# Setting up a pair of heads' operands behind the newest exponential, with the doubled copies on GpSimd

## The chip, the cores and the metric

The kernel runs on one core of one Trainium2 chip. The metric is the device time of one execution in microseconds (us). The profiler's names for the engines are used throughout: PE is TensorE (matmuls and transposes), PEld its weight loads, ACT is ScalarE, DVE is VectorE, POOL is GpSimd, and SP is SyncE, which only issues DMAs. Each engine works through its own instructions in order. POOL also issues the DMAs of its own queue, among them all gathers from the paged cache.

## The reference

One step of a decoder layer is computed for two groups that share weights: a prompt of 1024 tokens, and eight samples of one token each, which attend to 8192 cached tokens. The parts that matter here are the prompt's:

```python
q, k, v, logf, u, z = mixer_inputs(rmsnorm(xp, g_mix[l]), w_in[l], b_f[l], g_sgu_v[l])
xp = xp + merge_heads(fox_prompt(q, k, v, logf), sgu_prompt(u, z, w_s[l], b_s[l]),
                      g_att_out[l], g_sgu_out[l], w_o[l])
...
    s = jnp.einsum('bqhd,bkhd->bhqk', q, k).astype(jnp.float32) * (ATT_HEAD_DIM ** -0.5)
    s = s + (cq.astype(jnp.float32).transpose(0, 2, 1)[:, :, :, None]
             - ck.astype(jnp.float32).transpose(0, 2, 1)[:, :, None, :])
    s = jnp.where(kpos[None, :] <= qpos[:, None], s, -jnp.inf)
    p = jax.nn.softmax(s, axis=-1).astype(v.dtype)
```

There are eight heads of width 64, each with a cumulated forget gate `c` that enters the scores as a difference. Beside the attention stands a gating unit, `u * (W z + b)`, whose output is normalised by the mean of its squares. After both come an output projection, a cross-attention into 256 memory tokens, and a gated MLP.

## The kernel before, in words

The prompt is worked in stages: the input projection (`p1`), attention for the first 512 query rows (`attention(0)`), attention for the second 512 (`attention(1)`), and then, for each half, output projection, cross-attention and MLP. Beside attention of the first half, a filler generator computes the memory's keys and values (`pmem`) and the gating unit (`gating(0)`). `gating(1)` runs beside the first half's cross-attention. The decode of the samples is a background generator: a loop at the end of `build` advances it by one step whenever the main generator's yields have added up to a pace, which is 20 in the first half's attention. A step is, among other things, a gather of keys (L1354), their multiplication with the query and a sum (DVE, L1360 and L1364), and a gather of values (L1413) with matmuls (L1419).

The program's text order is not the engines' order. The framework simulates the program and orders every engine's instructions by when they become ready in that simulation, the earlier in the text first. `tc.issue_after(x)` forbids one thing: the instructions of its block may not stand ahead of `x` on `x`'s engine. `newest(e)` gives the newest instruction traced on an engine, and `behind(e)` is `issue_after` with the newest instruction of engine `e` at the main program's last yield.

Attention works on pairs of heads (`hp`, four per half), each in two blocks (`blk`) of 256 query rows, with four score tiles per block (two heads `j`, two row tiles `ii`). A score tile is a full-precision product made of two matmuls over split operands (L759, L761), plus a mask (L763). Its maximum is taken by DVE (L765, or L768 where the tile fills two PSUM banks), and the exponential with its row sum by ACT (L766, L769). The probabilities are transposed by PE (L787) and copied out of PSUM by ACT or DVE (L792, L794), and multiplied with the values (L803); the result is turned back (L823, L825). The program keeps two score tiles ahead of their transposition.

The operands of a pair come from `setup`, a generator with one yield. Its first part transposes the queries (L701) into a PSUM tile. For each head it copies the high part out twice by ACT (L707 into `qq[0:64, 0]`, L708 into `qq[0:64, 1]`), fetches the gate's rows by POOL's DMAs (L709, L721), and lets DVE subtract the high part from the PSUM tile to get the low part (L724). Its second part does the same with the keys: transposes (L729), a copy by ACT (L733), a second copy into the other 64 partitions, by ACT in the first half of the sequence (L737) and by POOL in the second (L735), and DVE's subtraction (L740). In the first half, POOL then stores both key parts to DRAM (`ks_d`, L743 and L744), from which the second half reads them. In the main loop, `setup` of the next pair starts after the last score tile of block 0 and ends one score tile later.

The first pair of each half has no pair before it. For the first half, `early` in the input projection runs the load and the whole setup; for the second half, `late` does so when pair 3 (`at`) of the first half begins. In the second half, `late` issues the loads for the following stage.

The gating unit takes the sum of squares of each of its four row tiles by ACT (`ssq_into`, L228, called once `u` has been formed), and normalises with it.

Of the kernel before, what the change touches and what calls it, by code (L numbers as in the profile page):

```python
# [7 lines left out]
F32 = mybir.dt.float32  # L8
# [3 lines left out]
AF = mybir.ActivationFunctionType  # L12
# [6 lines left out]
P = 128  # L19
# [59 lines left out]
def build(nc, tc, ctx, a, phases=None):  # L79
# [145 lines left out]
    def ssq_into(dst, src):  # L225
        n = src.shape[-1]
        j = tpool.tile([P, 1024], BF16, tag="junk", bufs=1, name=nm("junk"))[: src.shape[0], :n]
        nc.scalar.activation(j, src, AF.Square, accum_out=dst)  # L228
# [354 lines left out]
    def gating(hf):  # L583
# [6 lines left out]
        for pr_ in range(2):  # L590
# [32 lines left out]
                    )  # L623
                yield 1
            for i in range(2):
                ssq_into(ssu[:, pr_ * 2 + i : pr_ * 2 + i + 1], u[:, i, :])
            us_.append(u)
        r = rstd_of(ssu, AW, 4, "r4")
        yield 1
# [51 lines left out]
    def attention(hf, late=None, at=3):  # L681
# [14 lines left out]
            return qn, kn, vn  # L696

        def setup(hp, qn, kn, vn):
            tr = (MS, BB, BA)[SB]()
            for i in range(4):  # L700
                nc.tensor.transpose(tr[:, i * P : (i + 1) * P], qn[:, i, :], ident)  # L701
            qab, ka, kb = [], [], []
            for j in range(2):
                h = hp * 2 + j
                rows = slice(64 * j, 64 * j + 64)
                qq = U([P, 2, 512], F32R)
                nc.scalar.activation(qq[0:64, 0, :], tr[rows, :], AF.Copy)  # L707
                nc.scalar.activation(qq[0:64, 1, :], tr[rows, :], AF.Copy)  # L708
                nc.gpsimd.dma_start(qq[64:68, 1, :], cq_d[h, :, hf * 512 : (hf + 1) * 512])  # L709
                qab.append(qq)  # L710
                if hf == 0:
# [10 lines left out]
            for j, qq in enumerate(qab):  # L722
                rows = slice(64 * j, 64 * j + 64)
                nc.vector.tensor_tensor(qq[64:128, 0, :], tr[rows, :], qq[0:64, 0, :].bitcast(F32), op=ALU.subtract)  # L724
            for kh in (hf,):
                yield
                tr = (MS, BB, BA)[SB]()
                for i in range(4):
                    nc.tensor.transpose(tr[:, i * P : (i + 1) * P], kn[:, i, :], ident)  # L729
                s = slice(kh * 512, kh * 512 + 512)  # L730
                for j in range(2):
                    rows = slice(64 * j, 64 * j + 64)
                    nc.scalar.activation(ka[j][0:64, s], tr[rows, :], AF.Copy)  # L733
                    if KP & 1 << hf:
                        nc.gpsimd.tensor_copy(ka[j][64:128, s], ka[j][0:64, s].bitcast(F32))  # L735
                    else:
                        nc.scalar.activation(ka[j][64:128, s], tr[rows, :], AF.Copy)  # L737
                for j in range(2):
                    rows = slice(64 * j, 64 * j + 64)
                    nc.vector.tensor_tensor(kb[j][0:64, s], tr[rows, :], ka[j][0:64, s].bitcast(F32), op=ALU.subtract)  # L740
            if hf == 0:
                for j in range(2):
                    nc.gpsimd.dma_start(ks_d[hp * 2 + j, :, 0, :], ka[j][0:64, :].bitcast(F32))  # L743
# [3 lines left out]
        def scores(qkv, ls, blk, j, ii):  # L747
# [16 lines left out]
            if nch == 1:  # L764
                nc.vector.tensor_reduce(mx, s, axis=AX.X, op=ALU.max, negate=True)  # L765
                nc.scalar.activation(p_[:, :e], s, AF.Exp, bias=mx, accum_out=ls[:, ii, j : j + 1])  # L766
            else:
                nc.vector.tensor_reduce(mx, both, axis=AX.XY, op=ALU.max, negate=True)  # L768
                nc.scalar.activation(  # L769
                    p_[:, :e].rearrange("p (c n) -> p c n", c=2), both, AF.Exp, bias=mx, accum_out=ls[:, ii, j : j + 1]  # L770
                )
            return p_

        turns = [0.0, 0]
# [61 lines left out]
                queue.pop(0)()  # L836

        got = []
        for _ in setup(0, *load(0)):
            pass  # L840
        nxt = None
        yield 2
        for hp in range(4):
            for _ in nxt or ():
                pass
            qkv, nxt = got.pop(), None
            if hp == at and late:
                late()
            for blk in range(2):
                ls = sm([P, 2, 2], "ls", 3)  # L850
                pt = []
                nkt = hf * 4 + blk * 2 + 2
# [430 lines left out]
    def final(hf, xt, sq):  # L1283
# [7 lines left out]
                nc.sync.dma_start(a["o_y"][rows, c], xt[i][:, c])  # L1291
        yield 1

    last = {}
    bgs, acc, phase = [], [0.0], ["p1", None]

# [660 lines left out]
```

## Time and profile before

| | us |
|---|---|
| median of 3 runs | 1864.72 (1860.55 to 1866.24) |
| the profiled execution's own time | 1858.95 |
| its span, first to last instruction | 1857.2 |
| PE busy | 1779.9 |
| DVE busy | 1390.5 |
| ACT busy | 749.2 |
| POOL busy | 488.5 |
| attention, both halves | 265 to 512 |
| PE busy in attention | 211.92 of 247.00 |

A row of the profile names the source line, the engine, the operation, and the output and input tiles. In the view of waits, "A <- B" says that A's engine stood idle until B ended, with the total, the number of times and the longest. In the timeline each row has the start, the duration and, in brackets, the idle time before it and who ended it. In the view by windows each engine's busy time in a stretch is given with its number of instructions, then the clock that PE was granted as a share of full speed, and the DMA engines' share.

### The profile page before, as it was taken

The numbers are of one execution on the slowest core, as the hardware profiler recorded it, in microseconds if no ns is written. First come the engines' busy times: TensorE is split into PE (matmuls) and PEld (weight loads), VectorE is DVE, ScalarE is ACT, GpSimd is POOL, SyncE is SP. The second block draws the span as 40 slices with busy tenths as digits, with TensorE's granted clock in tenths as the row PEclk, the third lists the DMA queues.
The fourth block names the chain that finished last, engine by engine and source line by source line (L and its number), as shares of the span: only waits on it lengthen the run. The fifth ranks groups of instructions, "written<-read, shape, count | busy, mean of one in ns | idle before, by whom it ended". The sixth has DMA issues, their size and how long they took to land.

```text
span 1857.2 us, 24238 instructions
## 1 busy us (share of the span) xinstructions
PE 1779.9 (96%) x9239; PEld 1290.3 (69%) x9239; DVE 1390.5 (75%) x1666; ACT 749.2 (40%) x1365; POOL 488.5 (26%) x437
## 2 busy tenths in 40 slices
PE   8999998878998999999999999999999999999998
PEld 5887666556676757777777777766576668767765
DVE  4788567876688787989989899898975549754344
ACT  6332355565633535332324234235353334232232
POOL 1243342242122222224332232233322111111110
PEclk9999999999999999999999999999999999999999
DMA  8877889684596976768768789988879588577971
GB/s 318 291 268 262 311 302 346 230 255 150 187 400 228 349 258 262 278 249 326 293 246 339 269 312 363 360 308 338 332 275 348 198 298 266 199 270 265 342 277 60
DMA packets 157012, 521.27 MB, mean 281 GB/s; under 512 B 20808, under 2 KB 40520, under 8 KB 124128
## 3 DMA queue, kind: packets, MB, share of 16 engines
q0 software_dynamic: 57168, 341.14, 49.0%
q1 hardware_dynamic: 92816, 165.99, 25.6%
q10 hardware_dynamic: 6912, 12.59, 1.8%
q8 instruction: 73, 1.20, 0.3%
q14 instruction: 43, 0.35, 0.1%
HBM read 495.73 MB, written 23.93 MB: 280 GB/s over the span
## 4 chain that ended last, share of the span: by engine, by line
PE 67%; DVE 10%; issue 9%; DMA 9%; ACT 4%; POOL 2%; SPq 0%; POOLq 0%; DVEq 0%; ACTq 0%
PE ba L270 9%; PE ba L271 9%; PE ba L272 9%; PE dv L1419 5%; PE bb L271 5%; PE bb L270 4%; PE bb L272 4%; DMA kv<-cache_v,kidx 2%; DVE kv L1360 2%; DMA kv<-cache_k,kidx 2%; DVE s L1364 2%; PE ba L1008 1%; DVE wl L234 1%; PE ba L1010 1%; PE ba L1009 1%
## 5 line engine op out<-in xcount | busy, mean ns | idle before, releaser
L233 ACT ACTIVATE wh<-wr 128x1024 fp32r<-128x1024 f32 (+2 forms) x220 | 229.0, 1044 | 493.1 <-PE ba L271 159.3
L234 DVE TENSOR_TENSOR wl<-wr,wh 128x1024 fp32r<-128x1024 f32 (+2 forms) x220 | 262.2, 1200 | 142.2 <-PE ba L272 54.5
L1354 POOL DMA_INDIRECT kv<-cache_k,kidx x128 | 185.3, 1448 | 611.5 <-DVE s L1364 376.6
L1360 DVE TENSOR_TENSOR kv<-kv,d 128x1024 f32<-128x1024 f32 (+1 forms) x185 | 295.6, 1628 | 42.6 <-DMA kv<-cache_k,kidx 42.5
L1364 DVE TENSOR_REDUCE s<-kv 128x16 f32<-128x1024 f32 (+1 forms) x185 | 295.9, 1619 | 0.1
L1413 POOL DMA_INDIRECT kv<-cache_v,kidx x128 | 171.3, 1338 | 294.4 <-PE dv L1419 191.9
L271 PE MATMUL ba<-u,wh 128*128 128x512 f32 (+1 forms) x560 | 220.6, 394 | 2.3 <-DVE u L237 2.1
L270 PE MATMUL ba<-u,wh 128*128 128x512 f32 (+1 forms) x560 | 219.8, 394 | 1.3 <-ACT u L236 1.1
L272 PE MATMUL ba<-u,wl 128*128 128x512 f32 (+1 forms) x560 | 219.7, 393 | 0.0
L270 PE MATMUL ba<-wh,u 128*128 128x512 f32 (+1 forms) x495 | 185.6, 378 | 1.4 <-DVE u L740 1.0
L271 PE MATMUL ba<-wl,u 128*128 128x512 f32 (+1 forms) x495 | 186.3, 377 | 0.0
L272 PE MATMUL ba<-wh,u 128*128 128x512 f32 (+1 forms) x495 | 184.2, 376 | 0.0
L1419 PE MATMUL dv<-kv,s 128*32 128x512 f32 x1024 | 130.5, 618 | 7.0 <-DMA kv<-cache_v,kidx 6.8
L270 PEld LDWEIGHTS ba<-u,wh 128*128 128x128 f32 x560 | 106.0, 190 | 33.8 <-issue 9.3
L271 PEld LDWEIGHTS ba<-u,wh 128*128 128x128 f32 x560 | 106.4, 190 | 33.1 <-issue 7.1
L272 PEld LDWEIGHTS ba<-u,wl 128*128 128x128 f32 x560 | 106.3, 190 | 32.5 <-issue 10.1
L271 PE MATMUL bb<-u,wh 128*128 128x512 f32 (+1 forms) x304 | 118.2, 389 | 1.7 <-DVE u L237 1.7
L270 PE MATMUL bb<-u,wh 128*128 128x512 f32 (+1 forms) x304 | 118.0, 389 | 0.5 <-ACT u L236 0.5
L272 PE MATMUL bb<-u,wl 128*128 128x512 f32 (+1 forms) x304 | 116.8, 384 | 0.0
L270 PEld LDWEIGHTS ba<-wh,u 128*128 128x128 f32 x495 | 92.9, 188 | 26.5 <-issue 5.9
L271 PEld LDWEIGHTS ba<-wl,u 128*128 128x128 f32 x495 | 93.1, 188 | 22.2 <-issue 5.9
L272 PEld LDWEIGHTS ba<-wh,u 128*128 128x128 f32 x495 | 93.1, 188 | 19.9 <-issue 3.1
(437 smaller groups left out, 3197.5 us busy)
## 6 DMA issues: line engine op xcount, KB each, us to landing
wr<-w_up SPq DMA_DIRECT2D x88, 512.0 KB
kv<-w_up POOLq DMA_DIRECT2D x22, 1024.0 KB, 7.0
wr<-w_down SPq DMA_DIRECT2D x40, 512.0 KB
kv<-w_down POOLq DMA_DIRECT2D x11, 1024.0 KB, 8.0
wr<-w_in SPq DMA_DIRECT2D x16, 512.0 KB
wr<-w_o SPq DMA_DIRECT2D x16, 512.0 KB
wr<-w_cq SPq DMA_DIRECT2D x16, 512.0 KB
wr<-w_co SPq DMA_DIRECT2D x16, 512.0 KB
```

What stands on the lines that cost most here:

```text
L233: nc.scalar.activation(h, src, AF.Copy)
L234: nc.vector.tensor_tensor(l, src, h.bitcast(F32), op=ALU.subtract)
L270: mmul(out, sh, mh, start=(i == 0), stop=False)
L271: mmul(out, sh, ml, start=False, stop=False)
L272: mmul(out, sl, mh, start=False, stop=(i == n - 1))
L1008: mmul(pss[i], mh[k][:, tb], wh, start=(k == korder[0]), stop=False)
L1009: mmul(pss[i], mh[k][:, tb], wl, start=False, stop=False)
L1354: nc.gpsimd.indirect_dma_start(kv, None, a["cache_k"], off(kidx[:, b, ch : ch + 1]))
L1360: nc.vector.tensor_tensor(kvv[:, i : i + m, :], kvv[:, i : i + m, :], qb.unsqueeze(1).broadcast_to((P, m, 512)), op=ALU.mult)
L1364: nc.vector.tensor_reduce(s[:, ch * 4 + i : ch * 4 + i + m, :].rearrange("p k h -> p (k h)"), kvv[:, i : i + m, :].rearrange("p k (h d) -> ...
L1413: nc.gpsimd.indirect_dma_start(kv, None, a["cache_v"], off(kidx[:, b, ch : ch + 1]))
L1419: mmul(dv[32 * j : 32 * j + 32, :], s[:, ch * 4 : ch * 4 + 4, :].rearrange("p k h -> p (k h)"), kvv[:, j, :], start=(ch == 1), stop=(ch == ...
```

## The change

`lastexp` is a list that holds the newest exponential's instruction; `scores` refreshes it. The diff does these things:

- The transposes of `setup` stand behind the newest PE instruction of the main program's last yield.
- ACT's copies in `setup` (L707, L733) stand behind the newest exponential, if there is one.
- The second query copy (L708) and the first half's second key copy (L737) are made by POOL, from the first copy in SBUF instead of from PSUM. The second half's key copy was made so before.
- The squares of the gating unit stand behind the newest exponential, if there is one.
- The first pair's setup yields 2 between its query part and its key part. `early` therefore runs only the query part within the input projection, and the key part comes at the start of attention. `late` is called in both blocks of pair 3 of the first half, so that the second half's first setup has its query part in block 0 and its key part in block 1.

```diff
             for i in range(2):
-                ssq_into(ssu[:, pr_ * 2 + i : pr_ * 2 + i + 1], u[:, i, :])
+                with tc.issue_after(lastexp[0]) if lastexp else nullcontext():
+                    ssq_into(ssu[:, pr_ * 2 + i : pr_ * 2 + i + 1], u[:, i, :])
...
         def setup(hp, qn, kn, vn):
-            tr = (MS, BB, BA)[SB]()
-            for i in range(4):
-                nc.tensor.transpose(tr[:, i * P : (i + 1) * P], qn[:, i, :], ident)
+            calm = lambda: tc.issue_after(lastexp[0]) if lastexp else nullcontext()
+            with behind(ENG.PE):
+                tr = (MS, BB, BA)[SB]()
+                for i in range(4):
+                    nc.tensor.transpose(tr[:, i * P : (i + 1) * P], qn[:, i, :], ident)
             qab, ka, kb = [], [], []
             for j in range(2):
                 h = hp * 2 + j
                 rows = slice(64 * j, 64 * j + 64)
                 qq = U([P, 2, 512], F32R)
-                nc.scalar.activation(qq[0:64, 0, :], tr[rows, :], AF.Copy)
-                nc.scalar.activation(qq[0:64, 1, :], tr[rows, :], AF.Copy)
+                with calm():
+                    nc.scalar.activation(qq[0:64, 0, :], tr[rows, :], AF.Copy)
+                nc.gpsimd.tensor_copy(qq[0:64, 1, :], qq[0:64, 0, :].bitcast(F32))
                 nc.gpsimd.dma_start(qq[64:68, 1, :], cq_d[h, :, hf * 512 : (hf + 1) * 512])
...
-            for kh in (hf,):
-                yield
+            yield
+            with behind(ENG.PE):
                 tr = (MS, BB, BA)[SB]()
                 for i in range(4):
                     nc.tensor.transpose(tr[:, i * P : (i + 1) * P], kn[:, i, :], ident)
-                s = slice(kh * 512, kh * 512 + 512)
-                for j in range(2):
-                    rows = slice(64 * j, 64 * j + 64)
+            s = slice(hf * 512, hf * 512 + 512)
+            for j in range(2):
+                rows = slice(64 * j, 64 * j + 64)
+                with calm():
                     nc.scalar.activation(ka[j][0:64, s], tr[rows, :], AF.Copy)
-                    if KP & 1 << hf:
-                        nc.gpsimd.tensor_copy(ka[j][64:128, s], ka[j][0:64, s].bitcast(F32))
-                    else:
-                        nc.scalar.activation(ka[j][64:128, s], tr[rows, :], AF.Copy)
-                for j in range(2):
-                    rows = slice(64 * j, 64 * j + 64)
-                    nc.vector.tensor_tensor(kb[j][0:64, s], tr[rows, :], ka[j][0:64, s].bitcast(F32), op=ALU.subtract)
+                nc.gpsimd.tensor_copy(ka[j][64:128, s], ka[j][0:64, s].bitcast(F32))
+            for j in range(2):
+                rows = slice(64 * j, 64 * j + 64)
+                nc.vector.tensor_tensor(kb[j][0:64, s], tr[rows, :], ka[j][0:64, s].bitcast(F32), op=ALU.subtract)
...
+            lastexp[:] = [newest(ENG.Activation)]
             return p_
...
         got = []
-        for _ in setup(0, *load(0)):
+        first = setup(0, *load(0))
+        next(first)
+        yield 2
+        for _ in first:
             pass
         nxt = None
         yield 2
...
             qkv, nxt = got.pop(), None
-            if hp == at and late:
-                late()
             for blk in range(2):
+                if hp == at and late and (blk == 0 or hf == 0):
+                    late()
                 ls = sm([P, 2, 2], "ls", 3)
...
+    lastexp = []
     last = {}
```

## The prediction

> **What bounds the kernel now.** I read the page's engine table first, then the busy time by windows, then TensorE's waits in the one stage that the change touches, then the timeline at each of those waits.
>
> ```profile
> span 1857.2 us, 24238 instructions
> PE 1779.9 (96%) x9239; PEld 1290.3 (69%) x9239; DVE 1390.5 (75%) x1666; ACT 749.2 (40%) x1365; POOL 488.5 (26%) x437
> ```
>
> TensorE (PE) is busy for 96% of the span. Without removing matmuls there are about 77 us of idle time to win, and whatever the clock loses. The view by windows, first for attention as a whole (both halves, 265 to 512 us), then for its worst stretch, where one half passes into the other:
>
> ```profile
> core 0: us, PE busy (x) PEld busy (x) DVE busy (x) ACT busy (x) POOL busy (x), PEclk, DMA share, GB/s
> 265.00:512.00 247.00, 211.92 (x1317) 148.45 (x1316) 179.58 (x267) 148.22 (x328) 68.46 (x80) 0.94 0.71 244
> 365.00:396.00 31.00, 24.01 (x131) 14.29 (x133) 21.32 (x41) 19.16 (x54) 10.38 (x14) 0.83 0.71 224
> ```
>
> In attention PE idles 247.0 - 211.9 = 35.1 us, nearly half of all its idle time, and a granted clock of 0.94 costs up to 0.06 x 247 = 14.8 us more (0.17 x 31 = 5.3 us of it in the worst stretch). GpSimd (POOL) works only 68.5 of those 247 us. Whom PE waits for, in the view of waits of this window (total, times, longest):
>
> ```profile
> PE bb L787 <- ACT t L766: 8.3, 6, 2.7
> PE ba L759 <- ACT wr L769: 5.9, 4, 2.6
> PE ms L803 <- ACT t L794: 5.4, 4, 2.1
> ...
> PE bb L803 <- ACT u L794: 2.2, 3, 1.1
> ```
>
> These are 21.8 of the 35.1 us. Each names ScalarE (ACT): an exponential (L766, L769) or the copy of turned probabilities (L794) that came late. ACT works in order, so the question is what stood ahead of it.
>
> **The change part by part.** *Work taken from ACT.* The doubled query copy L708 goes to POOL for all pairs, the doubled key copy L737 for the first half (the second half has it on POOL already, L735). The groups by line, for 225 to 515 us, and the POOL copy's row:
>
> ```profile
> L708 ACT ACTIVATE u<-ba 64x512 fp32r<-64x512 f32 x16 | 9.3, 583 | 0.0
> ...
> L737 ACT ACTIVATE u<-ba 64x512 fp32r<-64x512 f32 x8 | 4.7, 592 | 0.2
> ```
>
> ```profile
> L735 POOL CAST u<-u x8: 603/607/2821, 379.6 to 471.6; 64x512 fp32r<-64x512 f32 x8
> ```
>
> So ACT loses 9.3 + 4.7 = 14.0 us and POOL gains 24 x 0.607 = 14.6 us. Since only two ACT copies then read the transposed PSUM tile before VectorE's (DVE's) subtraction, that tile comes free about 2 x 0.583 = 1.2 us earlier too. What this is worth is read at the waits. The clearest is the start of the second half, where six setup copies stand ahead of an exponential:
>
> ```profile
> 377.86 0.59 ACT L707 ACTIVATE u<-ba 64x512 fp32r<-64x512 f32 x1 [2.40 <-PE ba L701]
> ...
> 380.42 0.59 ACT L733 ACTIVATE u<-ba 64x512 fp32r<-64x512 f32 x1
> 381.03 0.37 ACT L766 ACTIVATE t<-ba,mx 128x128 f32<-128x128 f32 x1
> ```
>
> ```profile
> 378.55 0.79 DVE L765 TENSOR_REDUCE mx<-ba 128x1 f32<-128x128 f32 x2 [0.73 <-PE ba L763]
> ```
>
> ```profile
> 381.55 0.48 PE L787 MATMUL bb<-cp,t 128*128 128x128 f32 x1 [2.67 <-ACT t L766]
> ...
> 384.53 0.78 PE L759 MATMUL ba<-u,u 128*128 128x512 f32 x1
> ```
>
> The maxima of the first of the two scores were there at about 378.55 + 0.79/2 = 378.9, the exponential began at 381.03: 2.1 us late, of PE's 2.67. Here all the edits act together: two of the copies go to POOL, the others queue behind the newest exponential, and the key part of this setup moves to the next block. The other waits of this kind, PE's rows:
>
> ```profile
> 303.82 0.47 PE L270 MATMUL ba<-wh,u 128*128 128x512 f32 x1 [0.95 <-DVE u L740]
> 331.87 0.55 PE L787 MATMUL bb<-cp,t 128*128 128x128 f32 x3 [0.58 <-ACT t L766]
> 361.91 0.44 PE L787 MATMUL bb<-cp,t 128*128 128x128 f32 x2 [1.24 <-ACT t L766]
> 406.98 1.30 PE L803 MATMUL bb<-u,u 128*64 128x256 f32 x10 [1.08 <-ACT u L794]
> 437.55 1.95 PE L803 MATMUL ms<-u,u 128*64 128x256 f32 x16 [1.86 <-ACT t L794]
> 467.08 1.73 PE L803 MATMUL bb<-u,u 128*64 128x256 f32 x13 [0.89 <-ACT u L794]
> ```
>
> and an example of what stands ahead, at 437:
>
> ```profile
> 435.63 0.59 ACT L707 ACTIVATE u<-ba 64x512 fp32r<-64x512 f32 x1
> 436.13 0.58 ACT L708 ACTIVATE u<-ba 64x512 fp32r<-64x512 f32 x1
> 436.74 0.60 ACT L794 ACTIVATE u<-bb 128x512 f32<-128x512 f32 x1
> ```
>
> Each such setup puts two L708 of 0.58, together 1.17 us, ahead of the late copy, so I credit the smaller of the wait and 1.17: 0.95 + 0.58 + 1.17 + 1.08 + 1.17 + 0.89 = 5.8. With the 2.1 above, **7.9 us of waits** go. What is late next is DVE's maximum, for which the exponentials of the second half already wait:
>
> ```profile
> ACT wr L769 <- DVE mx L768: 17.0, 17, 1.9
> ```
>
> so I credit no more than the copies' own time.
>
> *The gating unit's squares* (L228, four in each half) only move behind the newest exponential. Their chain ends in a store that is read much later; the 1.24 us above already holds what their move can give: nothing extra.
>
> *The clock.* Behind the 2.67 us gap the 512-column score took 0.78 us; one at full clock took 0.47:
>
> ```profile
> 362.54 0.47 PE L759 MATMUL ba<-u,u 128*128 128x512 f32 x1
> ```
>
> If the gap goes, I take half of the worst stretch's 5.3 us back: **2.6 us**. Bounds: 0 (other gaps keep the clock down), and 14.8 for all of attention.
>
> The Trainium skill ("TensorE: Matmul & The Clock Gate", "What's actually happening") says that the clock halves after an idle window of some 3.4 us. By that rule a gap of 2.67 us would cost no clock and its removal would give none back: the sum would be 2.6 us smaller. The trace disagrees here, by its clock of 0.83 behind that gap, unless several short gaps add up.
>
> *The POOL copies as a new wait.* The query copy is now ACT, then POOL, then the scores' second matmul. Its slack, from the last L708 of a setup to the first score of the next pair:
>
> ```profile
> 330.26 0.59 ACT L708 ACTIVATE u<-ba 64x512 fp32r<-64x512 f32 x1
> ```
>
> ```profile
> 340.42 0.31 PE L759 MATMUL ba<-u,u 128*128 128x128 f32 x1
> ```
>
> 9.6 us: a copy of 0.6 us, even two, hides. But POOL also issues the cache gathers in order, and a gather holds the queue until its buffer is free:
>
> ```profile
> 458.06 0.98 POOL L1413 DMA_INDIRECT kv<-cache_v,kidx  x1 [15.40 <-DVE s L1364]
> ```
>
> A copy queued behind that one would be 15.4 - 9.6 = 5.8 us late. The other way round, a gather, or the constants' DMAs (L709, L721) behind a copy that waits for ACT, can slip; POOL's 178 idle us cover that. Copies also stretch:
>
> ```profile
> 412.75 2.82 POOL L735 CAST u<-u 64x512 fp32r<-64x512 f32 x1
> ```
>
> ```profile
> 412.75 2.34 DVE L1360 TENSOR_TENSOR kv<-kv,d 128x1024 f32<-128x1024 f32 x2
> ```
>
> One of eight did, beside the decode's multiply: 24/8 x 2.2 = 6.6 us of POOL, again under its idle time. The Trainium skill ("GPSIMD Engine Reference", "Key points") states this contention for DVE instructions with two SBUF inputs; the trace agrees, with 2.82 against 0.61 us. Between 0 and 5.8 us I take **1 us**, nearest to the eight L735 of which none was held by a gather.
>
> *The first setup's key part* moves from the projection's tail to the start of attention, with its four stores to ks_d on POOL and behind PE's newest matmul. Rows of the same operations:
>
> ```profile
> 377.66 0.60 PE L729 MATMUL ba<-cp,t 128*128 128x128 f32 x4
> ```
>
> ```profile
> L740 DVE TENSOR_TENSOR u<-ba,u 64x512 fp32r<-64x512 f32 x14 | 9.6, 685 | 6.7 <-POOL u L735 3.8 <-ACT u L733 2.7
> ```
>
> Its chain is the transposes (0.60), two ACT copies (2 x 0.59) and two DVE subtractions (2 x 0.69): 3.2 us before the first score. The memory projection's matmuls cover it, and PE then stood for DMA anyway:
>
> ```profile
> 271.50 2.50 PE L1419 MATMUL dv<-kv,s 128*32 128x512 f32 x12 [3.35 <-DMA kv<-cache_v,kidx]
> ```
>
> Without that cover it is 3.2 us; I take **1 us**. The added step of 2 in the main program's pace draws one block of the memory projection ahead and 0.1 of a decode step: nothing, at the same matmul count. The setup transposes' pin behind PE's newest matmul costs nothing where PE already ran them there.
>
> Sum: -7.9 - 2.6 + 1 + 1 = -8.5 us. The profiled execution took 1858.95 us and would take 1850.5; the runs' median of 1864.72 lies 5.8 us above it, and moves alike: **1856 us**.
>
> **The rivals.** *Copies caught behind gathers (slower).* The last POOL copies ahead of the gather that waited 15.4 us, and what all eight waited for:
>
> ```profile
> 441.43 1.23 POOL L735 CAST u<-u 64x512 fp32r<-64x512 f32 x2 [0.83 <-ACT u L733]
> ```
>
> ```profile
> POOL u L735 <- ACT u L733: 14.8, 5, 6.7
> ```
>
> These copies happened to be ahead. With 16 more copies in that queue, if two are caught at 5.8 us each, the loss is 11.6 against a gain of 8.5, and the exponentials' new place makes those operands later still, so part of the gain (I take 4 us) is all that stays: +7.6, about 1872 us. It decides as soon as a copy stands behind a gather for more than 9.6 us. Against it: all of L735's waits are for ACT. *The exponential is not the limit (no change).* Between two exponentials stand DVE's maximum and the decode's products on the same engine; the 17.0 us of ACT's waits for L768 speak for it, the rows that name L708 ahead of a late copy against it. Then only the 2.1 us at 381 and some 2 us of PSUM time come, less 2 us of costs: -2, 1863 us. *The waits go, the clock does not come back:* -7.9 + 2 = -5.9, 1859 us.
>
> **How the numbers follow.** A measurement of this kernel tells about 0.3%, 5.6 us, from no change. Forecast 0.40, faster; waits without clock 0.13, just faster; no change 0.18; slower 0.29. That makes faster 0.53, same 0.18, slower 0.29. The range's low end is 7.9 us of waits with 10.6 of the 14.8 us of clock at no cost, 1846; the high end is the slower rival's 1872. The likeliest case by itself spans 1850 to 1860 us.
>
> **What would show it.** Right: L708 and L737 gone from ACT, 24 more POOL copies of 0.61 us, PE's waits for L766 and L794 in attention down from 15.9 to about 9 us, and the clock near 396 us above 0.9. Wrong: new waits of PE's L761 or L759 for the POOL copies, a copy just behind a gather that waited over 9.6 us, PE idle at the start of attention over 3.35 us before the first score, or the same PE waits now named after DVE.

## The result, and the profile after

The changed kernel took 1872.65 us in the median of eight runs (1870.56 to 1875.77), the kernel before 1865.7 us beside it. The ratio is 1.0043, with a 95% interval of 1.0031 to 1.0056: about 8 us slower (0.0043 x 1866). The forecast was faster, 1856 us. One caution for all the traces below: the profiled execution of before (1858.95 us) was faster than all eight of its runs and that of after (1875.77 us) was the slowest of its own, so the two traces differ by more than the kernels do. A second profiled execution of the kernel before, 1873.86 us, stands among the experiments for that reason.

The engine table of the page after:

```profile
span 1874.0 us, 24258 instructions
PE 1790.1 (96%) x9239; PEld 1297.2 (69%) x9239; DVE 1393.3 (74%) x1664; ACT 736.5 (39%) x1341; POOL 503.6 (27%) x461
```

Read against the same two lines of before: 24 instructions and 12.7 us are gone from ACT, POOL has 24 more and 15.1 us. The diff did what it says. Then the view by windows, attention as a whole and its worst stretch (columns as in the prediction):

```profile
265.00:512.00 247.00, 207.32 (x1268) 144.91 (x1262) 176.57 (x261) 134.42 (x302) 83.68 (x104) 0.91 0.70 231
365.00:396.00 31.00, 23.28 (x134) 14.03 (x134) 24.40 (x48) 18.32 (x54) 17.50 (x21) 0.83 0.73 235
```

PE idles 39.7 us in attention instead of 35.1, the clock is 0.91 instead of 0.94, and the worst stretch still has 0.83. Whom PE waits for in this window:

```profile
PE bb L792 <- ACT t L770: 12.9, 8, 8.0
PE ba L763 <- DVE u L744: 4.3, 2, 3.5
PE bb L828 <- ACT t L817: 4.2, 3, 2.9
PE ba L763 <- ACT wr L773: 3.3, 4, 1.3
PE ms L808 <- ACT u L799: 2.5, 4, 0.7
PE ba L706 <- DMA t<-q_d: 2.4, 1, 2.4
```

(L770 and L773 are the exponentials, L799 the copy of turned probabilities, L744 the keys' subtraction, L817 the copy of the result.) Two things are to be seen. About half of the waits that the prediction wanted gone are gone: for the exponential of one bank and the copies, 12.9 + 2.5 = 15.4 us are left, but 8.0 of them are a single new one, so 7.4 remain of the 15.9 that the prediction counted (with the small rows of the same kind, 9.1 of 17.6: the same fall of 8.5). And there are new ones: the single wait of 8.0, and the rows for L744, L817 and q_d, of which the same view of before has little:

```profile
PE ba L759 <- DVE u L740: 1.9, 2, 1.0
...
PE ba L701 <- DMA t<-q_d: 1.0, 1, 1.0
...
PE bb L823 <- ACT t L812: 0.9, 2, 0.5
```

On the other side, the 3.4 us that PE waited for the gather of `cache_v` in before (271.50, in the prediction) have no counterpart in after.

The wait of 8.0 is at the start of the first half. First the kernel before there: its first score (PE), the only split of a memory weight between that score and the first exponential (L233), and that exponential, in the timeline:

```profile
264.21 0.33 PE L759 MATMUL ba<-u,u 128*128 128x128 f32 x1
...
269.64 1.06 ACT L233 ACTIVATE wh<-wr 128x1024 fp32r<-128x1024 f32 x1 [2.62 <-DMA wr<-w_ck]
...
272.62 0.37 ACT L766 ACTIVATE t<-ba,mx 128x128 f32<-128x128 f32 x1
```

The same in the kernel after, from the timelines of PE, DVE and ACT:

```profile
273.26 0.22 PE L763 MATMUL ba<-u,u 128*128 128x128 f32 x1
...
285.93 0.47 PE L792 MATMUL bb<-cp,t 128*128 128x128 f32 x1 [7.98 <-ACT t L770]
```

```profile
276.73 0.62 DVE L769 TENSOR_REDUCE mx<-ba 128x1 f32<-128x128 f32 x2
```

```profile
276.19 1.06 ACT L233 ACTIVATE wh<-wr 128x1024 fp32r<-128x1024 f32 x1 [2.97 <-DMA wr<-w_ck]
283.05 1.06 ACT L233 ACTIVATE wh<-wr 128x1024 fp32r<-128x1024 f32 x1 [5.80 <-DMA wr<-w_ck]
284.13 1.28 ACT L770 ACT_TABLE_LOAD   x1
285.42 0.37 ACT L770 ACTIVATE t<-ba,mx 128x128 f32<-128x128 f32 x1
```

The scores come 9 us later: the late keys and a whole block of the memory projection now stand ahead of them (with the late keys alone, e13 below, the first score is at 268.8). Their maxima are ready at about 277, but ACT works in order and still has two weight splits ahead of the exponential, and each waits for its weights. (By ACT's timeline eight splits of `w_ck` stand ahead of the first exponential in after, and five in before.) So the exponential stands behind a DMA that has nothing to do with it, until 285.4, and PE with it. The clock falls in that stretch (view by windows, PE alone: us, PE busy, granted clock, DMA share, GB/s), before and after:

```profile
262.00:300.00 38.00, 29.68 (x148) 0.91 1.03 400
```

```profile
262.00:300.00 38.00, 26.42 (x125) 0.74 0.86 315
286.00:300.00 14.00, 10.40 (x38) 0.50 0.62 205
```

The first exponential is 12.8 us later than before. By the fifth exponential the delay is down to 5.0 us, since the block that was drawn ahead need not be done there: the two kernels of the table below with that block (after, e11) take 17 us from the first to the fifth, the others 24 to 29. At the last exponential 5.2 us are left. The starts of the 1st, 5th, 21st, 33rd and 64th exponentials in the timelines of nine profiled executions (the 33rd is the first of the second half):

| kernel | 1st | 5th | 21st | 33rd | 64th | span |
|---|---|---|---|---|---|---|
| before | 272.6 | 297.4 | 366.6 | 396.7 | 500.0 | 1857.2 |
| before, second execution | 271.5 | 298.9 | 373.2 | 402.0 | 505.9 | 1872.0 |
| after | 285.4 | 302.4 | 369.2 | 403.5 | 505.2 | 1874.0 |
| e5, pins alone | 273.6 | 297.2 | 368.1 | 396.7 | 495.7 | 1864.7 |
| e10, first setup whole, gains early | 269.9 | 298.5 | 371.9 | 399.6 | 500.1 | 1865.9 |
| e11, the change, gains early | 285.2 | 302.2 | 366.5 | 403.0 | 508.0 | 1871.3 |
| e13, late keys, nothing drawn | 272.7 | 299.0 | 375.5 | 405.7 | 504.9 | 1861.1 |
| e14, as e10, copies on ScalarE | 274.5 | 298.7 | 365.9 | 393.9 | 494.4 | 1858.6 |
| e18, e14 again | 271.3 | 298.1 | 364.0 | 392.3 | 490.3 | 1853.0 |

What lies behind the last exponential takes 1357 us in one execution of the kernel before and 1366 in the other. A single trace therefore tells where attention loses, and only the repeated runs tell how much a kernel loses.

### The profile page after: what moved, and what is told of

Same layout as the page of the kernel before. It is cut to its first block, busy times and chain, and to the rows that moved or that the text cites. A ratio compares the mean times of both kernels' runs of the same rounds, so it can differ in the third digit from the quotient of the medians.

```text
span 1874.0 us, 24258 instructions
## 1 busy us (share of the span) xinstructions
PE 1790.1 (96%) x9239; PEld 1297.2 (69%) x9239; DVE 1393.3 (74%) x1664; ACT 736.5 (39%) x1341; POOL 503.6 (27%) x461
## 4 chain that ended last, share of the span: by engine, by line
PE 58%; DMA 6%; issue 4%; DVE 4%; ACT 1%; POOL 1%; POOLq 0%; DVEq 0%; ACTq 0%; SPq 0%
PE ba L270 9%; PE ba L272 9%; PE ba L271 9%; PE bb L270 4%; PE bb L272 4%; PE bb L271 4%; PE dv L1429 4%; DMA kv<-cache_v,kidx 2%; PE dv L1693 1%; DMA kv<-cache_k,kidx 1%; PE ba L1017 1%; PE ba L1018 1%; PE ba L1019 1%; DVE kv L1370 1%; DVE s L1374 1%
## 5 line engine op out<-in xcount | busy, mean ns | idle before, releaser
L233 ACT ACTIVATE wh<-wr 128x1024 fp32r<-128x1024 f32 (+2 forms) x220 | 228.9, 1044 | 483.6 <-PE ba L271 151.7
L234 DVE TENSOR_TENSOR wl<-wr,wh 128x1024 fp32r<-128x1024 f32 (+2 forms) x220 | 262.1, 1199 | 141.5 <-PE ba L272 56.6
L1364 POOL DMA_INDIRECT kv<-cache_k,kidx x128 | 190.5, 1488 | 584.0 <-DVE s L1374 392.8
L1374 DVE TENSOR_REDUCE s<-kv 128x16 f32<-128x1024 f32 (+1 forms) x184 | 294.9, 1625 | 0.0
L1423 POOL DMA_INDIRECT kv<-cache_v,kidx x128 | 172.1, 1345 | 272.7 <-PE dv L1429 165.4
```

Of the source, the lines that this page charges most:

```text
L233: nc.scalar.activation(h, src, AF.Copy)
L234: nc.vector.tensor_tensor(l, src, h.bitcast(F32), op=ALU.subtract)
L1364: nc.gpsimd.indirect_dma_start(kv, None, a["cache_k"], off(kidx[:, b, ch : ch + 1]))
L1374: nc.vector.tensor_reduce(s[:, ch * 4 + i : ch * 4 + i + m, :].rearrange("p k h -> p (k h)"), kvv[:, i : i + m, :].rearrange("p k (h d) -> ...
L1423: nc.gpsimd.indirect_dma_start(kv, None, a["cache_v"], off(kidx[:, b, ch : ch + 1]))
```

## The experiments

**First series: which part of the change costs.** Theory A: the start of the first half. Theory B: the copies in GpSimd's queue.

e1_whole0, the change with the first half's first setup whole in the projection, as before:

```diff
         first = setup(0, *load(0))
-        next(first)
-        yield 2
+        if hf:
+            next(first)
+            yield 2
         for _ in first:
             pass
```

> The changed kernel, but the first pair of the first half has its whole setup in the input projection, as before. Theory A (the start): the step of 2 between query and key part draws a block of the memory projection ahead of the first scores; ScalarE's first exponential then stands behind weight splits (L233) that wait for a saturated DMA, and PE idles 8 us and runs at half clock afterwards. By it this kernel loses that idle time, its first exponential comes at about 272 us as before (285 in the changed kernel), and it takes 1858 to 1862 us, below the kernel before. Theory B (GpSimd): the copies on GpSimd's queue make the operands late. By it nothing but the start changes and it stays at 1869 to 1873 us.

Measured: 1.0023 (1.0004 to 1.0043), 1870.72 us: the first exponential is at 269.9, early as theory A has it, but the time is in theory B's range.

e2_nodraw, the change with the keys still late, but no memory block drawn ahead in the first half:

```diff
             pass
         nxt = None
-        yield 2
+        yield 2 if hf else 0
```

> The changed kernel with its key part still at the start of attention, but the step that follows this part draws no block of the memory projection (a yield of 0 in place of 2, in the first half alone). It separates two causes inside theory A. If the block drawn ahead is the cause, the first exponential has one split of w_ck ahead of it instead of four, comes at about 273 us, and the kernel takes 1858 to 1863 us. If the key part's own chain (about 3 us of transposes, copies and subtractions at the start) is the cause, the 8 us of idle time stay and it takes 1870 to 1873 us. Theory B: 1870 to 1873 us.

Measured: 1.0014 (0.9998 to 1.0030), 1871.0 us; the first exponential at 272.5, as theory A has it, and again theory B's time.

e3_split0, the kernel before with nothing but the split of the first half's first setup:

```diff
-        for _ in setup(0, *load(0)):
+        first = setup(0, *load(0))
+        if hf == 0:
+            next(first)
+            yield 2
+        for _ in first:
             pass
```

> The kernel before with one edit: the first pair's key part of the first half comes at the start of attention, with the added step of 2. All copies stay on ScalarE, nothing is pinned. Theory A: the loss comes without any other part of the change, 1873 to 1879 us, with a PE wait of 5 us or more for the first exponential. Theory B: no copies on GpSimd, so 1864 to 1868 us, as before.

Measured: 1.0042 (1.0027 to 1.0056), 1874.21 us, theory A's time. Its PE wait for the first exponential is 4.3 us, not 5 or more, and that exponential (282.35) is held by another engine than in after. Its splits are done early enough, but its maximum stands on DVE behind the low parts of two splits (L234) and a sum of the decode (L1368). ACT, then DVE:

```profile
282.35 0.37 ACT L766 ACTIVATE t<-ba,mx 128x128 f32<-128x128 f32 x1 [4.02 <-DVE mx L765]
```

```profile
277.45 2.35 DVE L234 TENSOR_TENSOR wl<-wr,wh 128x1024 fp32r<-128x1024 f32 x2
279.73 2.27 DVE L1368 TENSOR_REDUCE s<-kv 128x32 f32<-128x2048 f32 x1
```

e4_pool, the kernel before with nothing but the doubled copies on GpSimd:

```diff
-KP = 2
+KP = 3
...
-                nc.scalar.activation(qq[0:64, 1, :], tr[rows, :], AF.Copy)
+                nc.gpsimd.tensor_copy(qq[0:64, 1, :], qq[0:64, 0, :].bitcast(F32))
```

> The kernel before with one edit: the doubled query copy and the first half's doubled key copy are made by GpSimd (24 copies). Nothing is pinned or split. Theory A: the 14 us taken from ScalarE pay, 1858 to 1863 us. Theory B: the copies on GpSimd's queue are the loss, 1869 to 1874 us, with PE waiting for them or for a gather behind them.

Measured: 1.0001 (0.9985 to 1.0016), 1866.94 us, between the two theories.

What follows: the split alone makes the whole loss (e3), so theory A has the place. Without it, though, e1 and e2 are not faster than before, and copies alone are worth nothing. The relief of ScalarE, which the prediction counted at 7.9 us, was given back somewhere.

**Second series: where the relief goes.** The traces of e1, e2 and e4 share one new gap. The gating unit multiplies by a row of gains, `g_sgu_v`, whose load (L585) takes a small work tile and so waits for one to come free. In e1, from the timelines of SP's queue, DVE and PE:

```profile
351.78 0.34 SPq L585 DMA_DIRECT2D t<-g_sgu_v  x1
```

```profile
361.46 2.74 DVE L598 SCALAR_TENSOR_TENSOR u<-u,rz,t 128x512 f32<-128x512 f32 x4 [4.79 <-DMA t<-g_sgu_v]
```

```profile
362.93 3.72 PE L606 MATMUL ba<-u,u 128*128 128x128 f32 x16 [5.45 <-DVE u L598]
```

In the first profiled execution of the kernel before, the load leaves at 346.26 and PE waits 1.32 us, with the 16 products in 2.05 us where e1's take 3.72. This gave theory G (the gain went into that late load; whether it lands in time is what the expectations call a race), against theory C (whatever is taken from ScalarE comes back as the next late operand).

e5_pins, the kernel before with only the pins of the setups' transposes and copies; copies on ScalarE, squares free, first setups whole:

```diff
+            calm = lambda: tc.issue_after(lastexp[0]) if lastexp else nullcontext()
+            with behind(ENG.PE):
                 tr = (MS, BB, BA)[SB]()
...
+                with calm():
                     nc.scalar.activation(qq[0:64, 0, :], tr[rows, :], AF.Copy)
                     nc.scalar.activation(qq[0:64, 1, :], tr[rows, :], AF.Copy)
```

> The kernel before with the setups' transposes, q copy and k copy held behind the newest exponential, both copies still on ScalarE, the first setup whole, the gating unit's squares free. Theory C (every wait taken from ScalarE's queue comes back as a wait of the setup's followers): ratio 0.999 to 1.0015, the first exponential at 272.6 us as before, no more than 2 us gained between it and the last. Theory D (the pins earn what the prediction said, and the GpSimd copies and the start lose it): 5 to 8 us faster, ratio 0.9957 to 0.9973, the last exponential 5 to 8 us earlier than before.

Measured: 1.0026 (1.0010 to 1.0043), though the profiled execution had its last exponential 4.2 us earlier than before. That is above both theories, and the cause was not settled: the profiled execution (1866.67 us) was near the fast end of 1865 to 1877.

e6_gsv, the kernel before with the gains in a constant tile:

```diff
-NT = 7
+NT = 6
...
-        gs8 = T2()[:8]
-        nc.sync.dma_start(gs8, a["g_sgu_v"].broadcast_to((8, 512)))
+        nc.sync.dma_start(gsvc, a["g_sgu_v"].broadcast_to((P, 512)))
+        gs8 = gsvc[:8]
...
-        gsv = T2()
-        nc.sync.dma_start(gsv, a["g_sgu_v"].broadcast_to((P, 512)))
+        gsv = gsvc
```

> The kernel before with the gating unit's row of gains g_sgu_v held in a constant tile that is loaded in the projections, and one small work tile fewer (6 for 7) to make room. It is the control for the next run. The 1.3 us that TensorE waits for the gating unit's first product should fall by at most 1.3: ratio 0.9990 to 1.0005. If the missing work tile costs, 1.001 to 1.003.

Measured: 1.0032 (1.0017 to 1.0046), just above both expectations; what its trace shows is told at e9.

e7_whole0_gsv, e1 with the same constant tile:

> The changed kernel with the first half's first setup whole again (as e1_whole0) and the gains in a constant tile as in e6_gsv. Theory G (in e1_whole0 the gain went into the late load of the gains, 5.45 us of TensorE's wait and the half clock behind it): some 5 us faster than e1_whole0, ratio to before 0.999 to 1.000. Theory C (the wait only moves on to the next late operand): ratio stays at 1.002, the last exponential within 1.5 us of e1_whole0's.

Measured: 1.0012 (0.9994 to 1.0029). This is 6 us below its control e6 in the medians (1867.01 against 1873.27 us), 4 us by the ratios, with one tile fewer in both. It lies between theory G's range and theory C's 1.002, with the last exponential 2.5 us before e1's (497.7 against 500.2).

e8_before_again, the kernel before:

> The kernel before, unchanged, for a second profiled execution: its first (1858.95 us) was the fastest run of eight. First exponential within 1 us of 272.6, TensorE's wait for the gating unit's first product 1.3 to 5 us: near 1.3 if the late load of the gains belongs to the change, near 5 if it is part of this kernel's own spread.

Measured: 1873.86 us, and PE's row at the gating unit's first product is

```profile
359.89 3.78 PE L606 MATMUL ba<-u,u 128*128 128x128 f32 x16 [4.50 <-DVE u L598]
```

Its load of the gains, in SP's timeline:

```profile
348.01 0.34 SPq L585 DMA_DIRECT2D t<-g_sgu_v  x1
```

It left at 348.01 instead of 346.26. So 1.75 us more at the issue went with 3.2 us more of waiting, and with products at half the speed (3.78 us for 16 against 2.05). The kernel before has this wait in some executions; the change did not make it. In DVE's row the profile names another DMA (`cq_d`) as the last to land; it names the gains in e1, e2 and e4 (4.70 to 4.79 us).

**Third series: the same with the gains loaded early, all seven tiles kept.** The edit, in all four kernels:

```diff
         for w, dst in ((a["w_ck"], mk_d), (a["w_cv"], mv_d)):
+            if dst is mv_d:
+                gains.append(T2())
+                nc.sync.dma_start(gains[0], a["g_sgu_v"].broadcast_to((P, 512)))
...
     def gating(hf):
-        gsv = T2()
-        nc.sync.dma_start(gsv, a["g_sgu_v"].broadcast_to((P, 512)))
+        gsv = gains.pop() if gains else T2()
+        if hf:
+            nc.sync.dma_start(gsv, a["g_sgu_v"].broadcast_to((P, 512)))
```

e9_early, the kernel before with it:

> The kernel before with the gating unit's load of the gains issued ahead of the second half of the memory projection, into a small work tile that it then keeps, all seven tiles as before. It is the control of the next three. TensorE's wait for the gating unit's first product, 1.3 us in one profiled execution of the kernel before and 4.5 in the other, should be at most 1.3 each time. Theory G (that wait is a race that the kernel before loses in some executions): 1 to 4 us faster, ratio 0.998 to 0.9995. If the tile held longer holds up the queries' loads: 1.000 to 1.002.

Measured: 1.0033 (1.0020 to 1.0046), slower, outside both expectations. The wait for the gains is gone, and another has come, in the view of waits of SP's queue and the timelines of SP and PE:

```profile
SPq L637 <- DVE u L636: 21.5, 2, 21.2
```

```profile
371.70 0.55 SPq L693 DMA_DIRECT2D t<-q_d  x1
```

```profile
384.19 1.12 PE L706 MATMUL ba<-cp,t 128*128 128x128 f32 x4 [5.78 <-DMA t<-q_d]
```

With the gating unit earlier in the planned order, its store (L637, `sgn_d`) stands ahead of the second half's first query load on SP, waits 21 us for DVE, and holds the query load from 363.98 (before) to 371.70. e6 has the same wait, 5.71 us. For the kernel before it is as theory C has it: the wait moves on.

e10_whole0_early, e1 with the early gains:

> The changed kernel with the first half's first setup whole (as e1_whole0) and the early load of the gains (as e9_early). Theory G (in e1_whole0 the gain went into the lost race for the gains): 4 to 7 us faster than e1_whole0, ratio to before 0.997 to 0.999, below e9_early by 2 us or more: what the pins earn. Theory C (the wait only moves on): ratio 1.001 to 1.003, and not below e9_early.

Measured: 0.9981 (0.9967 to 0.9994), faster, and 7 us below e1 in the medians, as theory G has it. Here the planned order keeps the query load ahead of that store.

e11_change_early, the changed kernel with the early gains:

> The changed kernel with only the early load of the gains added, its split start left in. Theory A (the loss is made at the start of the first half): the first exponential at 285 us again, 12 to 13 us later than before, and the ratio 1.003 to 1.005, 5 us or more above e10_whole0_early. If the lost race was the cause of the whole: ratio 1.000 or below.

Measured: 1.0048 (1.0032 to 1.0065), 11.9 us above e10 in the medians (1875.62 against 1863.72), and the two differ in the split of the first half alone. Its start is that of after, from the timelines of ACT and PE:

```profile
282.85 1.06 ACT L233 ACTIVATE wh<-wr 128x1024 fp32r<-128x1024 f32 x1 [5.32 <-DMA wr<-w_ck]
283.93 1.28 ACT L775 ACT_TABLE_LOAD   x1
285.22 0.37 ACT L775 ACTIVATE t<-ba,mx 128x128 f32<-128x128 f32 x1
```

```profile
285.73 0.47 PE L797 MATMUL bb<-cp,t 128*128 128x128 f32 x1 [7.61 <-ACT t L775]
```

e12_nosplit_early, e10 with the second half's first setup whole too:

> The changed kernel with both first setups whole and the early load of the gains: the pins, the GpSimd copies and the squares' pin are what is left of the change. The prediction's 2.1 us for the start of the second half go with the split: by it, 2 us slower than e10_whole0_early. If that part earns nothing: within 1.5 us of it.

Measured: 0.9986 (0.9974 to 0.9998), 1 us from e10.

**Fourth series: what of the split costs, and what earns.**

e13_late_keys, e11 without the drawn block (the edit of e2):

> As e11_change_early, the first half's keys still set up late, but without the block of the memory projection drawn ahead. If the drawn block and the four weight splits that it puts ahead of the first exponential on ScalarE are the whole loss: first exponential at 272 to 273.5 us and the ratio within 0.001 of e10_whole0_early's 0.998. If the late keys cost by themselves: first exponential at 272 to 273.5 us as well, but 3 us or more above e10, ratio 1.000 to 1.002.

Measured: 0.9984 (0.9965 to 1.0003), e10's value. The late keys cost nothing that can be seen in the time, though PE waits 2.44 us ahead of the first score for a key copy on GpSimd (268.83). The drawn block is the loss, 0.0048 + 0.0016 = 0.0064 or 12 us.

e14_copies_on_scalare, from e10:

```diff
                 with calm():
                     nc.scalar.activation(qq[0:64, 0, :], tr[rows, :], AF.Copy)
-                nc.gpsimd.tensor_copy(qq[0:64, 1, :], qq[0:64, 0, :].bitcast(F32))
+                    nc.scalar.activation(qq[0:64, 1, :], tr[rows, :], AF.Copy)
...
-                nc.gpsimd.tensor_copy(ka[j][64:128, s], ka[j][0:64, s].bitcast(F32))
+                if KP & 1 << hf:
+                    nc.gpsimd.tensor_copy(ka[j][64:128, s], ka[j][0:64, s].bitcast(F32))
+                else:
+                    with calm():
+                        nc.scalar.activation(ka[j][64:128, s], tr[rows, :], AF.Copy)
```

> As e10_whole0_early, but the doubled copies of q and of the first half's k back on ScalarE, each behind the newest exponential. If the copies earn nothing (e4_pool: 1.0001): ratio 0.997 to 0.999. If the relief of ScalarE by 16 copies of some 0.5 us is what e10 earns: 1.000 or above.

Measured: 0.9956 (0.9942 to 0.9971), better than both expectations. The copies on GpSimd cost in this kernel. The traces differ first at the start of the first half. PE's rows in e10, then in e14:

```profile
288.87 3.64 PE L1435 MATMUL dv<-kv,s 128*32 128x512 f32 x16 [5.07 <-DMA kv<-cache_v,kidx]
295.96 1.12 PE L711 MATMUL ba<-cp,t 128*128 128x128 f32 x4 [3.45 <-DMA t<-q_d]
```

```profile
271.73 3.57 PE L1439 MATMUL dv<-kv,s 128*32 128x512 f32 x16 [3.60 <-DMA kv<-cache_v,kidx]
...
292.41 3.47 PE L1439 MATMUL dv<-kv,s 128*32 128x512 f32 x16
295.81 0.66 PE L711 MATMUL ba<-cp,t 128*128 128x128 f32 x4
```

and the clock behind them (windows of PE alone), e10, then e14:

```profile
286.00:304.00 18.00, 11.68 (x45) 0.56 0.92 356
```

```profile
286.00:304.00 18.00, 14.23 (x70) 0.81 0.98 367
```

In e10 the second decode product comes where its gather has not landed, and the next pair's query load is late behind it. The pattern recurs: in the six kernels with a whole first setup and GpSimd copies (e1, e4, e7, e10, e12, e15) PE waits 5.07 to 5.65 us for `cache_v` near 289 and 2.76 to 3.67 us for `q_d` near 296, with a clock of 0.56 to 0.70 from 286 to 304. In the nine executions with the query copies on ScalarE (before twice, e5, e6, e9, e14, e16, e17, e18) the `cache_v` wait is 3.35 to 3.81 us near 271, the `q_d` wait at most 2.66, the clock 0.72 to 0.91. That this pattern is what costs the time is not shown. e4 has it and is as fast as before (1.0001), and e12 has it and is no slower than e17, which has not (0.9986 against 0.9996).

e15_free_squares, from e10:

```diff
-                with tc.issue_after(lastexp[0]) if lastexp else nullcontext():
-                    ssq_into(ssu[:, pr_ * 2 + i : pr_ * 2 + i + 1], u[:, i, :])
+                ssq_into(ssu[:, pr_ * 2 + i : pr_ * 2 + i + 1], u[:, i, :])
```

> As e10_whole0_early, but the gating unit's squares go onto ScalarE as early as they can. The prediction gave their pin one wait of 0.89 to 1.17 us: ratio 0.998 to 0.9995, some 1 us above e10. If they decide the order of the loads and stores behind the gating unit: 3 us or more above e10, 1.000 or more.

Measured: 0.9996 (0.9979 to 1.0013), 0.0015 above e10 with intervals that overlap.

**Fifth series: what e14 rests on.** e16_act_late_gains is e14 without the early load, e17_act_nosplit e14 with the second half's first setup whole:

> As e14_copies_on_scalare, without the early load of the gains: the changed kernel with the copies on ScalarE and the first half's first setup whole. Theory G (the late gains cost 4.5 to 5.5 us of TensorE's wait and the half clock behind it wherever the race is lost): 4 to 8 us slower than e14, ratio 0.998 to 1.000, the wait for the gating unit's first product 3 us or more. If that load no longer matters here: 0.995 to 0.997.

> As e14_copies_on_scalare, with the second half's first setup whole too. By the prediction's 2.1 us for the start of the second half: ratio 0.9965 to 0.9975. If that split earns nothing (e12 against e10: 1 us, inside the error): 0.9945 to 0.996.

Measured: 1.0003 (0.9986 to 1.0021) and 0.9996 (0.9980 to 1.0011). Both lose nearly all of e14's gain. For e16 that is theory G's number, but not by its mechanism: its profiled execution shows 0.57 us of wait at the gating unit's first product, not 3 or more:

```profile
358.40 2.05 PE L606 MATMUL ba<-u,u 128*128 128x128 f32 x16 [0.57 <-DVE u L598]
```

e17 is outside both expectations: 7 us are lost where 2.1 were expected, and its last exponential is only 1.1 us later than e14's.

e18_act_again is the program of e14 once more:

> The same program as e14_copies_on_scalare in another series. If its gain is its own: ratio 0.994 to 0.9975, the last exponential between 493 and 497 us. If e14's series was a lucky one: 0.9985 to 1.0005, like e16 and e17.

Measured: 0.9944 (0.9921 to 0.9966), 1855.72 us, the last exponential at 490.3, earlier than expected. The gain is the program's own, and this version beats both kernels. Its attention, in windows:

```profile
265.00:512.00 247.00, 215.83 (x1354) 0.97 0.75 257
365.00:396.00 31.00, 25.74 (x166) 0.94 0.76 240
```

PE idles 31.2 us, 3.9 fewer than before, and the clock is 0.97 and 0.94 in the two windows instead of 0.94 and 0.83.

## Why the prediction was wrong

**The step that failed** is a sentence in the part on the first setup: the added step of 2 "draws one block of the memory projection ahead and 0.1 of a decode step: nothing, at the same matmul count". It was measured at 12 us (e11 against e13), at 8 us together with the late keys on the kernel before (e3), and at 4 to 5 us between the versions with late gains (after at 1.0043 against e1 at 1.0023 and e2 at 1.0014), where the other side waits for the gains. The matmul count is the same indeed, and PE has no gap until 278. But the block brought its weight splits along. In after and e11 two of them stand ahead of the first exponential on ScalarE and wait for DMA, in a stretch in which the DMA share is 1.00 (262 to 286); in e3 their low parts stand ahead of its maximum on VectorE. The prediction's sign for this was PE idle over 3.35 us ahead of the first score. There is no such wait in after; its 7.98 us lie behind the first scores, where the prediction did not look. So the place was named and the path was not.

**The first setup's key part**, taken at 1 us, costs nothing that can be seen in the time (e13 against e10).

**The waits, 7.9 us:** right in size for those rows, which shrank from 15.9 to 7.4 us beside the new one of 8.0. Wrong in taking them for the sum. In after, the rows for L744, L817 and q_d come to 4.3 + 4.2 + 2.4 = 10.9 us, against 1.9 + 0.9 + 1.0 = 3.8 in before: 7.1 us of new waits beside the 8.0. The two longest lead to DVE. The 2.87 us for a copy of the result (L817) stand behind an exponential that waits for its maximum. The 3.45 us for the keys' subtraction (L744) stand behind a sum of the decode (L1374) and a scaling of the first half's result (L911). ACT's row, then DVE's, then PE's:

```profile
375.10 0.69 ACT L770 ACTIVATE t<-ba,mx 128x512 f32<-128x512 f32 x1 [3.00 <-DVE mx L769]
```

```profile
417.01 2.35 DVE L1374 TENSOR_REDUCE s<-kv 128x16 f32<-128x1024 f32 x2
419.27 1.78 DVE L911 TENSOR_SCALAR u<-u,rar 128x512 f32<-128x512 f32 x4
```

```profile
422.64 0.44 PE L763 MATMUL ba<-u,u 128*128 128x448 f32 x1 [3.45 <-DVE u L744]
```

The prediction asked "what is late next" and answered "DVE's maximum", but it subtracted nothing for it. So for this part the rival "no change" is borne out, by its own way: the exponential's neighbours on DVE. The slower rival's 1872 us is the measured time by luck alone. One copy on GpSimd did start 5.7 us after its source was ready, behind a gather (272.75), but PE waits for none of these copies directly in attention of after, and once for 0.9 us by way of DVE (476.55).

**The second half's start, 2.1 of these:** 1 us between e12 and e10, and 0.0040 or 7 us between e17 and e14. The sign was right; the size is open. The wait of 2.67 us from which it was read is still there with the pins alone (e5, below).

**The clock, 2.6 us:** not in after, whose worst stretch still has 0.83, with a gap of 2.87 us in it. In e14 and e18 the clock there is 0.94: 0.11 x 31 = 3.4 us, near the size that was taken. But that a gap of 2.67 us by itself costs the clock, as the prediction read it, is not borne out. e5 keeps such a gap and has 0.94, and e17 has no gap over 1.61 us and has 0.83 (PE's rows with the longest gap, and windows of PE alone), e5, then e17:

```profile
383.78 0.33 PE L794 MATMUL bb<-cp,t 128*128 128x128 f32 x1 [2.67 <-ACT t L772]
365.00:396.00 31.00, 23.54 (x146) 0.94 0.76 241
```

```profile
379.33 0.39 PE L772 MATMUL ba<-u,u 128*128 128x256 f32 x1 [1.61 <-ACT t L779]
365.00:396.00 31.00, 24.93 (x143) 0.83 0.72 210
```

So the size in e14 and e18 was met by luck, and what lowers the clock in this stretch stays open. The rule of the Trainium skill ("TensorE: Matmul & The Clock Gate", "What's actually happening"), which asks for an idle window of some 3.4 us, would have given none of it. The clock of 0.83 in before, after and e17 does not agree with that, unless several shorter gaps add up.

**The GpSimd copies, 1 us between 0 and 5.8:** mis-sized. They are worth nothing on the kernel before (e4), and cost 0.0025 to 0.0037 or 5 to 7 us beside the pins, the second half's split and the early gains (e10 against e14 and e18). Without that split they cost nothing (e12 at 0.9986 against e17 at 0.9996). So their price hangs on the rest of the edit, and by what way is open: with them the gathers and the query load come late at the start, but that goes with no loss in e4 and e12. What they cost in after itself was not measured.

**The squares:** taken at nothing. 0.0015, inside the error (e15).

**What stays open.** The pins, the second half's split and the early gains earn 8 to 10 us together with the copies on ScalarE (e14, e18), but the pins alone are 1.0026, and without the early gains or the split the gain is gone (e16, e17). The traces of attention don't hold these differences: e16 and e17 are 3.2 and 1.1 us behind e14 at the last exponential, and 9 and 7 us in the runs. The same holds for the drawn block: e11 is 12.5 us behind e13 at the first exponential, 3.1 us at the last, and 12 us in the runs. What is lost behind attention was not found. So that the block costs is shown, and how its delay reaches the end is not.

## What to carry to other kernels

A yield or a draw that "only moves work" moves that work's other engines too: ask which copies, splits and loads come along, and what they stand ahead of on an engine that works in order, above all while DMA is full. Relief of one engine is worth the waits it removes minus the next late operand, so follow each removed wait to the next engine, and to the loads, stores and gathers behind it in the queues. And compare part by part with repeated runs on both sides: here one part cost 4 to 12 us, another nothing or 5 to 7, by what stood beside it, and the rest with one load moved earned 8 to 10. None of this could be read from the sum.

## What was not expected of the hardware

After a PE gap of 8 us the granted clock was 0.50 for the following 14 us (286 to 300 in after), although PE was then busy for 10.4 of them. Another gap, of 2.4 us, ends at 294.39.

A gap of 2.67 us went with a clock of 0.83 over 365 to 396 in before and of 0.94 in e5, and 0.83 was seen in e17 with no gap over 1.61 us there.

A load that left 1.75 us later went with 3.2 us more of PE's wait and with 16 products at half speed, 3.78 against 2.05 us. The same program had either case in different executions. The wait alone does not tell: in e3 the 16 products took 3.68 us behind a wait of 1.69.

Moving one load earlier made the kernel before 6 us slower (0.0033). In its trace a store then stood ahead of another load in the same queue and waited 21 us.
